# Output and up products that begin with three blocks in step, mixers paced as one sequence, and the residual's load

## The chip, the cores and the metric

The kernel runs on one core of one Trainium2 chip. The metric is the time of one execution on the device in microseconds (us), median over several runs.

## What is computed

The reference is one decoder block over 2048 positions and a width of 1024, in float32. Cut to what matters here:

```python
h = rms_norm(x, norm1_g[l]) * (1 + sc1) + sh1
proj = h @ w_in[l]
...                                    # gated linear attention and dilated attention
mixed = jnp.concatenate([y_gla, y_att], axis=-1)
x = x + g1 * (mixed @ w_out[l])
h = rms_norm(x, norm2_g[l]) * (1 + sc2) + sh2
u = causal_depthwise_conv(h @ w_up[l], conv_w[l], conv_b[l])
u_gate, u_val = jnp.split(u, 2, axis=-1)
x = x + g2 * ((jax.nn.silu(u_gate) * u_val) @ w_down[l])
```

`sh1` to `g2` come from one small product of the condition vector with `w_ada`, 48 blocks of 128 columns.

## The kernel before

The 2048 positions are four chunks (`NCH`) of 512; the width of 1024 is eight channel blocks (`KD`) of 128. Each weight block and each activation is split into a rounded part and a remainder (`hi`, `lo`), and every product of two of them is three matmuls, in `mm3` (L281): hi by hi (L288), lo by hi or hi by lo (L289, L290). A weight block is loaded by the DMA queue of SyncE (SP) into one of two `wraw` buffers (L220), cast by ScalarE into one of three `whi` buffers (L226), and its remainder is formed by VectorE, or by GpSimd for every second up block, into one of three `wlo` buffers (L227). `plan` lists all weight blocks in the order of use, and `weights` keeps casts up to two blocks ahead of the product. The products accumulate in four banks of PSUM (`psg`); the mixers use four others (`psa`).

The stages of a chunk:

- `proj`: normalised input by `w_in`, 26 steps. For the eight blocks of attention heads, `qk` squares the product (L403), casts the squares (L405), forms their remainder on GpSimd (L406) and sums them over a head by a product with a block matrix (L411, L412). The last step of chunks 1 to 3 is a "wide" block W1 that holds all four banks; ScalarE's Tanh (L460) and VectorE (L461) empty them.
- `mix`: the two kinds of attention of the chunk, 68 steps. It reads from and writes to DRAM scratch; the last step of each attention head pair stores its output block (`stage`, L839, store L840).
- `outproj`: loads the eight output blocks of the mixer (L855), casts them (L857) and forms remainders (L859); eight output blocks `out0` to `out7`, each 8 channel blocks of 3 matmuls, gated and added to the residual by VectorE (L865). Then come the sum of squares (`norm_stats`: squares L360, sums L365, a product with `ones` L367, Ln and Exp L369, L370) and `norm_mod` (L380 to L384), which makes the input of `ffn`.
- `ffn`: 44 blocks by `w_up` (gate block f and value block f + 22 in turn), a convolution (L888 to L895), the gate (L899 to L905), and `down`: per group of four f, eight output blocks by `w_down`, added to the residual (L933). The last group of chunks 0 to 2 (group 5, two f) is put off as `tail` and done in the next chunk's `outproj`, between the statistics of the norm and `norm_mod`. The residual of that chunk has by then been stored to DRAM (L937) and is loaded again, block by block (L930), into the four buffers of the tags `y0` and `y1`.

`run` sets the order. Generators are stepped against each other: `beside(a, na, b, nb)` does na steps of a for nb steps of b, then the rest of a. First 27 steps of the projections, which go along with the `w_ada` blocks; then the mixer of chunk c beside what follows:

```python
beside(self.mix(0), 68, gemm, 76)
beside(self.mix(1), 68, chain(self.outproj(0), self.ffn(0)), 86)
```

and so on up to mixer 3 beside chunk 2 at 68 per 90 steps; chunk 3's `outproj` and `ffn` run alone. This is the order of the text only. A scheduler that simulates a timeline then sets the order of each engine's instructions, by what it believes to be ready, and so already moves matmuls of several blocks between each other. Each engine and the DMA queue of SP then work in that order: an instruction that waits holds up what stands behind it.

## Time and profile before

| | |
|---|---|
| median of 3 runs | 2672.51 us (2671.59 to 2675.07) |
| the profiled execution | 2676.88 us |
| its span | 2675.1 us |
| TensorE (PE) busy | 2595.0 us, 97% |
| VectorE (DVE) busy | 1891.1 us, 71% |
| ScalarE (ACT) busy | 1273.2 us, 48% |
| GpSimd (POOL) busy | 512.1 us, 19% |
| granted clock of TensorE | 0.989 |

The span is the time between the first and the last instruction of the profiled execution. Times in the profile are from its start. A row of the timeline gives start, length, engine, line, operation and tiles (written <- read); in brackets stands how long the engine was idle before, and what ended that. A row of the waits gives the total, the number and the longest. TensorE's length of a matmul holds its way through the array, so two that follow each other at full rate start closer together than each is long.

### The profile page before, as it was taken

Reading aid. Unit: us, or ns where it says so; the run is one execution under the profiler, and the core shown is the slowest. Engines: PE = TensorE matmul, PEld = TensorE weight load, DVE = VectorE, ACT = ScalarE, POOL = GpSimd, SP = SyncE. Lnnn points to the kernel's source line nnn. Section 1 sums busy time; section 2 is a strip of 40 time slices with the busy share of each in tenths; the row PEclk is TensorE's granted clock in tenths of the full one; section 3 lists DMA queues with packets and bytes.
Section 4 is the critical chain, followed back from the end, with each engine's and each line's share of the span. In section 5 each row is a group of like instructions: output and inputs, shape, how many; then the busy total and the mean of one; then the engine's idle time right before and its main releaser. Section 6 shows DMA issues by size and latency. Waiting matters only on the chain.

```text
span 2675.1 us, 46823 instructions
## 1 busy us (share of the span) xinstructions
PE 2595.0 (97%) x18152; PEld 2122.1 (79%) x18152; DVE 1891.1 (71%) x3756; ACT 1273.2 (48%) x2607; POOL 512.1 (19%) x308
## 2 busy tenths in 40 slices
PE   5988999999989999999999999999999999999999
PEld 3777878888768888888788788878888888788887
DVE  8676784665676866777887777778777766666665
ACT  3445556656645455443545444445455443433332
POOL 1142451212221311101231111022211110111110
PEclk9999999999989999999999999999999999999999
DMA  7868455554552244447434444643344445323222
GB/s 276 295 212 276 160 173 170 186 188 150 173 175 95 93 126 133 124 125 241 135 100 135 133 133 129 197 156 122 104 141 138 140 132 180 131 95 101 97 95 95
DMA packets 192127, 405.09 MB, mean 151 GB/s; under 512 B 19473, under 2 KB 70434, under 8 KB 190626
## 3 DMA queue, kind: packets, MB, share of 16 engines
q1 hardware_dynamic: 191906, 402.11, 46.0%
q8 instruction: 143, 2.34, 0.4%
q14 instruction: 78, 0.64, 0.1%
HBM read 339.12 MB, written 62.91 MB: 150 GB/s over the span
## 4 chain that ended last, share of the span: by engine, by line
PE 77%; DVE 5%; ACT 3%; DMA 2%; issue 1%; POOL 0%; SPq 0%; DVEq 0%; ACTq 0%; POOLq 0%
PE psg L288 22%; PE psg L289 22%; PE psg L290 22%; PE psa L719 2%; PE psa L699 2%; PE psa L821 2%; PE psa L557 1%; DVE wlo L227 1%; ACT whi L226 1%; PE psa L816 1%; PE psa L735 1%; ACT big L709 1%; PE psa L627 0%; PE psa L628 0%; DMA sq<-y 0%
## 5 line engine op out<-in xcount | busy, mean ns | idle before, releaser
L288 PE MATMUL psg<-hhi,whi 128*128 128x512 f32 x2040 | 808.7, 399 | 15.6 <-ACT hhi L382 9.0
L289 PE MATMUL psg<-hlo,whi 128*128 128x512 f32 x2040 | 805.6, 395 | 6.4 <-DVE hlo L384 5.0
L290 PE MATMUL psg<-hhi,wlo 128*128 128x512 f32 x2040 | 803.9, 395 | 0.0
L226 ACT CAST whi<-wraw 128x1024 fp32r<-128x1024 f32 (+1 forms) x391 | 409.6, 1049 | 402.5 <-PE psg L289 307.5
L227 DVE TENSOR_TENSOR wlo<-wraw,whi 128x1024 fp32r<-128x1024 f32 (+1 forms) x300 | 386.1, 1287 | 150.2 <-ACT whi L226 141.4
L227 POOL TENSOR_TENSOR wlo<-wraw,whi 128x1024 fp32r<-128x1024 f32 x91 | 223.7, 2459 | 1340.8 <-ACT whi L226 1138.9
L288 PEld LDWEIGHTS psg<-hhi,whi 128*128 128x128 f32 x2040 | 386.2, 190 | 104.8 <-ACT hhi L382 12.3
L289 PEld LDWEIGHTS psg<-hlo,whi 128*128 128x128 f32 x2040 | 386.4, 189 | 90.3 <-DVE hlo L384 9.8
L290 PEld LDWEIGHTS psg<-hhi,wlo 128*128 128x128 f32 x2040 | 386.5, 189 | 82.3 <-issue 2.0
L288 PE MATMUL psg<-ghi,whi 128*128 128x512 f32 x704 | 280.1, 398 | 0.0
L289 PE MATMUL psg<-glo,whi 128*128 128x512 f32 x704 | 277.1, 394 | 0.0
L290 PE MATMUL psg<-ghi,wlo 128*128 128x512 f32 x704 | 276.3, 392 | 0.0
L933 DVE SCALAR_TENSOR_TENSOR x<-psg,mod,x 128x512 f32<-128x512 f32 x192 | 142.7, 747 | 124.4 <-PE psg L290 120.2
L889 DVE SCALAR_TENSOR_TENSOR y<-psg,conv_w_sb,y 128x511 f32<-128x511 f32 x176 | 130.9, 744 | 88.2 <-ACT y L888 87.9
L288 PE MATMUL psg<-whi,hhi 128*128 128x512 f32 (+2 forms) x512 | 177.5, 353 | 10.5 <-DVE stg L461 7.0
L289 PE MATMUL psg<-wlo,hhi 128*128 128x512 f32 (+2 forms) x512 | 178.7, 349 | 7.2 <-DVE wlo L227 7.2
L290 PE MATMUL psg<-whi,hlo 128*128 128x512 f32 (+2 forms) x512 | 177.3, 349 | 0.0
L288 PEld LDWEIGHTS psg<-ghi,whi 128*128 128x128 f32 x704 | 132.5, 188 | 32.2 <-issue 4.5
L290 PEld LDWEIGHTS psg<-ghi,wlo 128*128 128x128 f32 x704 | 132.5, 188 | 28.4 <-issue 1.0
L289 PEld LDWEIGHTS psg<-glo,whi 128*128 128x128 f32 x704 | 132.7, 188 | 28.1 <-issue 2.1
L709 ACT ACTIVATE big<-big,nm 128x256 f32<-128x256 f32 (+1 forms) x256 | 122.4, 479 | 47.1 <-DVE nm L724 47.1
L581 POOL TENSOR_TENSOR pt<-kt,pt 128x512 f32<-128x512 f32 x56 | 92.4, 1650 | 264.2 <-ACT pt L578 186.5
(199 smaller groups left out, 3617.7 us busy)
## 6 DMA issues: line engine op xcount, KB each, us to landing
wraw<-in_w_up_dram SPq DMA_DIRECT2D x176, 512.0 KB, 3.3
wraw<-in_w_down_dram SPq DMA_DIRECT2D x88, 512.0 KB, 3.3
wraw<-in_w_ch_dram SPq DMA_DIRECT2D x48, 512.0 KB, 4.2
wada<-in_w_ada_dram SPq DMA_DIRECT2D x40, 512.0 KB, 5.0
v<-v SPq DMA_DIRECT2D x68, 256.0 KB, 5.1
wraw<-in_w_tokw_dram SPq DMA_DIRECT2D x32, 512.0 KB, 3.9
wraw<-in_w_out_dram SPq DMA_DIRECT2D x32, 512.0 KB, 4.0
sq<-in_xT_dram SPq DMA_DIRECT2D x48, 256.0 KB, 3.9
```

Of the source, the lines that this page charges most:

```text
L226: nc.scalar.copy(hi[:, :n], raw[:, :n])
L227: (nc.gpsimd if pool else nc.vector).tensor_tensor(lo[:, :n], raw[:, :n], hi[:, :n].bitcast(F32), op=ALU.subtract)
L288: nc.tensor.matmul(ps, wh, hh, start=first and k == 0, stop=False, skip_group_check=shared)
L289: nc.tensor.matmul(ps, wh, hl, start=False, stop=False, skip_group_check=shared)
L290: nc.tensor.matmul(ps, wl, hh, start=False, stop=k == n - 1, skip_group_check=shared)
L581: nc.gpsimd.tensor_tensor(kh, gk, df, op=ALU.mult)
L699: nc.tensor.matmul(at(i, hh, z), q[H[hh], i * P:(i + 1) * P], key(H[hh], i, z), start=True, stop=True, skip_group_check=True)
L709: nc.scalar.activation(t[:, lo:hi], t[:, lo:hi], AF.Exp, bias=nm[:, hh, g, i:i + 1], scale=2.0 ** -(h + 1), accum_out=dn[:, hh, g, i:i + 1])
L719: nc.tensor.transpose(ps[:n, i * P:(i + 1) * P], part(S[hh], i), self.C("id"))
L821: nc.tensor.matmul(out, lhsT, rhs, start=first[hh], stop=False, skip_group_check=True)
L889: nc.vector.scalar_tensor_tensor(y[:, 1:], ps[:, :T - 1], self.cw[:, 1, b:b + 1], y[:, 1:], op0=ALU.mult, op1=ALU.add)
L933: nc.vector.scalar_tensor_tensor(x1, ps, self.mod[:, 40 + cb:41 + cb], x1, op0=ALU.mult, op1=ALU.add)
```

## The change

Three parts.

The mixers become one sequence, class `Mixers`, that is stepped at a rate: 68/64 steps per step of the projections, and 68/90 per step of every chunk's `outproj` and `ffn`. A mixer no longer ends with its stage: when mixer 0 is done beside the projections, mixer 1 starts there. `upto` makes sure that a mixer is done before its output is used. Chunk 0's mixer output is loaded and cast (`mixed`) inside the last step of the last projection, before its banks are emptied.

`three` makes the first three blocks of the output product, and of the up product, together: the loop over the channel blocks is outermost, the three blocks lie inside it, the third two channel blocks behind. The squares of the norm are taken block by block in the loop over output blocks.

The residual of the put-off down product is loaded by `spare_x1`: four blocks at the start of the next chunk's `outproj`, and one more after each of the first four blocks is stored.

```diff
+class Mixers:
+    def __init__(self, mix):
+        self.gs = [mix(c) for c in range(NCH)]
+        self.at, self.acc = 0, 0.0
+    def one(self):
+        done = object()
+        while self.at < NCH and next(self.gs[self.at], done) is done:
+            self.at += 1
+    def step(self, rate):
+        self.acc += rate
+        while self.acc >= 1.0:
+            self.acc -= 1.0
+            self.one()
+    def upto(self, c):
+        while self.at <= min(c, NCH - 1):
+            self.one()
...
+    def three(self, names, hs):
+        pss = [self.pg() for _ in range(3)]
+        ws = [self.weights(*n, ahead=2 - i) for i, n in enumerate(names)]
+        for k in range(KD + 2):
+            for b, ps in enumerate(pss):
+                j = k - 2 * (b == 2)
+                if 0 <= j < KD:
+                    self.mm3(ps, ws[b][j:j + 1], hs[j:j + 1], j == 0, True)
+            if k in (2, 5):
+                yield
+        self.psd = pss
+    def outproj(self, c):
+        hs = self.hs_out.pop(c, None) or self.mixed(c)
         x1 = self.load_x(c)
+        if c:
+            for _ in range(4):
+                self.spare_x1(c - 1)
+        acc = None
+        yield from self.three([("w_out", cb) for cb in range(3)], hs)
         for cb in range(KD):
-            ps = self.pg()
-            self.mm3(ps, self.weights("w_out", cb), hs)
+            if cb < 3:
+                ps = self.psd[cb]
+            else:
+                ps = self.pg()
+                self.mm3(ps, self.weights("w_out", cb), hs)
             nc.vector.scalar_tensor_tensor(x1[cb], ps, self.mod[:, 16 + cb:17 + cb], x1[cb], op0=ALU.mult, op1=ALU.add)
-            yield
+            acc = self.square(acc, x1[cb])
+            if cb >= 2:
+                yield
-        rstd = self.norm_stats(lambda k: x1[k])
+        rstd = self.norm_end(acc)
...
+    def spare_x1(self, c):
+        cb = len(self.late)
+        t = self.up.tile([P, T], F32, name="x1", tag=f"y{cb % 2}")
+        self.nc.sync.dma_start(t, self.D[c]["x1"][cb])
+        self.late.append(t)
...
     def ffn(self, c):
+        yield from self.three([("w_up", b) for b in (0, NF, 1)], h2)
...
     def down(self, c, gj, pgs):
                 if gj == 5 and defer:
-                    x1 = self.up.tile([P, T], F32, name="x1", tag=f"y{cb % 2}")
-                    nc.sync.dma_start(x1, self.D[c]["x1"][cb])
+                    x1 = self.late[cb]
...
                     nc.sync.dma_start(A["outT"][c, cb], x1)
+                    if defer and cb < 4:
+                        self.spare_x1(c)
...
-            yield from self.proj(c, hs.pop(), (lambda: begin(c + 1)) if c < 3 else None, () if c else done)
+            yield from self.proj(c, hs.pop(), (lambda: begin(c + 1)) if c < 3 else into_out, () if c else done)
+
+        def into_out():
+            mixers.upto(0)
+            self.hs_out[0] = self.mixed(0)
...
-        beside(self.mix(0), 68, gemm, 76)
-        beside(self.mix(1), 68, chain(self.outproj(0), self.ffn(0)), 86)
-        beside(self.mix(2), 68, chain(self.outproj(1), self.ffn(1)), 86)
-        beside(self.mix(3), 68, chain(self.outproj(2), self.ffn(2)), 90)
-        for _ in chain(self.outproj(3), self.ffn(3)):
-            pass
+        mixers = Mixers(self.mix)
+        for _ in gemm:
+            mixers.step(68 / 64)
+        for c in range(NCH):
+            for _ in chain(self.outproj(c), self.ffn(c)):
+                mixers.step(68 / 90)
+            mixers.upto(c + 1)
```

What the scheduler makes of it stands in three places. The number of matmuls is the same. TensorE's order is the same up to the end of chunk 1's first wide block (879 instructions) and from the middle of chunk 2's put-off down product to the end (1541 instructions).

**First listing.** TensorE at the start of chunk 0's output product, before. `psg_7411`, `psg_7443` and `psg_7490` are the banks of out0, out1 and out2; `hhi_7385` is the cast mixer output of channel block 6 and `hhi_7391` that of block 7; L557 are score matmuls of mixer 1.

```order
L290 MATMUL psg_7490<-hhi_7385,wlo_7415 128x512
L557 MATMUL psa_7522<-kt_7475 32x32 x16
L557 MATMUL psa_7540<-kt_7475 32x32 x16
L557 MATMUL psa_7598<-pt_7562,pt_7563 32x32 x8
L557 MATMUL psa_7609<-pt_7562,pt_7563 32x32 x8
L557 MATMUL psa_7692<-pt_7624,pt_7625 32x32 x16
L557 MATMUL psa_7710<-pt_7624,pt_7625 32x32 x16
L288 MATMUL psg_7411<-hhi_7391,whi_7260 128x512
L288 MATMUL psg_7443<-hhi_7391,whi_7299 128x512
L288 MATMUL psg_7490<-hhi_7391,whi_7414 128x512
L289 MATMUL psg_7411<-hlo_7393,whi_7260 128x512
```

Before, all three output blocks stop ahead of channel block 7, and score matmuls stand there. The same engine after: the last rows of W1 (banks `psg_7548` and `psg_7549`, written in turn with two others), small matmuls of mixer 1, and the first row of out0 (`psg_7819`).

```order
L315 MATMUL psg_7548<-whi_7589,hlo_5754 128x512
L313 MATMUL psg_7549<-whi_7589,hhi_5752 128x512
L314 MATMUL psg_7549<-wlo_7590,hhi_5752 128x512
L315 MATMUL psg_7549<-whi_7589,hlo_5754 128x512
L688 MATMUL psa_7849<-consts_sb_458,pt_7793 128x128 x4
L688 MATMUL psa_7857<-consts_sb_458,pt_7798 128x128
L574 MATMUL psa_7901<-consts_sb_458,s16_7893 128x128 x3
L688 MATMUL psa_7857<-consts_sb_458,pt_7798 128x128
L574 MATMUL psa_7901<-consts_sb_458,s16_7893 128x128
L688 MATMUL psa_7857<-consts_sb_458,pt_7798 128x128 x2
L591 MATMUL psa_7944<-kt_7892 32x32 x3
L313 MATMUL psg_7819<-hhi_7725,whi_7643 128x512
```

Out0 now begins behind W1 and a few small matmuls of the next mixer. A few rows further on, at channel block 2 of out0 and out1 (`psg_7820`) and block 0 of out2 (`psg_7821`):

```order
L313 MATMUL psg_7819<-hhi_7737,whi_7643 128x512
L314 MATMUL psg_7819<-hlo_7739,whi_7643 128x512
L315 MATMUL psg_7819<-hhi_7737,wlo_7644 128x512
L313 MATMUL psg_7820<-hhi_7737,whi_7695 128x512
L314 MATMUL psg_7820<-hlo_7739,whi_7695 128x512
L315 MATMUL psg_7820<-hhi_7737,wlo_7696 128x512
L313 MATMUL psg_7821<-hhi_7725,whi_7824 128x512
L314 MATMUL psg_7821<-hlo_7727,whi_7824 128x512
```

The blocks go in turn by channel block, out2 behind the others, and no score matmul stands between them up to the end of all three.

**Second listing.** The DMA queue of SP between the store of mixer 0's last output block (L840) and its load for the output product (L855), before. `rg` is the scratch that W1 is stored to, `x` the residual.

```order
L840 DMA y_123<-stage 128x512
L465 DMA rg_154<-stg 128x512
L342 DMA x<-in_xT_dram 128x512 x2
L465 DMA rg_154<-stg 128x512
L342 DMA x<-in_xT_dram 128x512
L465 DMA rg_154<-stg 128x512
L342 DMA x<-in_xT_dram 128x512
L220 DMA wraw<-in_w_out_dram 128x1024
L682 DMA v_9577<-v_135 128x128 x2
L754 DMA v_9838<-v_135 128x512
L754 DMA v_9838<-v_122 128x512
L855 DMA sq<-y_123 128x512
```

The load stands eleven rows behind the store. After, around the last loads of mixer 0's output (L890); L499 stores W1:

```order
L462 DMA k_160<-o_7427 128x512
L890 DMA sq<-y_123 128x512 x2
L245 DMA wraw<-in_w_out_dram 128x1024
L890 DMA sq<-y_123 128x512
L245 DMA wraw<-in_w_out_dram 128x1024
L890 DMA sq<-y_123 128x512
L245 DMA wraw<-in_w_out_dram 128x1024
L367 DMA x<-in_xT_dram 128x512 x3
L499 DMA rg_154<-stg 128x512
L367 DMA x<-in_xT_dram 128x512
L691 DMA y_136<-stage 128x4x128
```

The loads of the mixer's output now stand ahead of the stores of W1 and of the residual's loads, and the store of mixer 0's last block (L874) stands 24 rows ahead of this piece.

**Third listing.** The same queue at the put-off down product of chunk 2, in chunk 3's output product, before: L935 stores a finished block, L930 loads the residual (`x_150` is the scratch).

```order
L935 DMA out_dram<-x_23008 128x512
L935 DMA out_dram<-x_23019 128x512
L935 DMA out_dram<-x_23030 128x512
L930 DMA x_23058<-x_150 128x512
L935 DMA out_dram<-x_23041 128x512
L930 DMA x_23069<-x_150 128x512
L930 DMA x_23080<-x_150 128x512
L930 DMA x_23091<-x_150 128x512
L935 DMA out_dram<-x_23058 128x512
```

After (L1011 stores, L939 loads):

```order
L1011 DMA out_dram<-x_22709 128x512
L1011 DMA out_dram<-x_22711 128x512
L1011 DMA out_dram<-x_22713 128x512
L939 DMA x_23018<-x_150 128x512
L1011 DMA out_dram<-x_22715 128x512
L939 DMA x_23029<-x_150 128x512
L939 DMA x_23040<-x_150 128x512
L939 DMA x_23051<-x_150 128x512
L1011 DMA out_dram<-x_23018 128x512
```

Nothing has moved: the load of the fifth block stands behind the stores of the first three, as before.

More of the change, by code (lines that the diff above doesn't have):

```diff
@@ L354, in norm_stats, with square, norm_end @@
     def norm_stats(self, src):
-        nc = self.nc
         acc = None
         for k in range(KD):
-            sq = self.tmp.tile([P, T], F32, name="sq", bufs=3)
-            nc.scalar.activation(sq, src(k), AF.Square)
-            if acc is None:
-                acc = self.tmp.tile([P, T], F32, name="rstd", bufs=2)
-                nc.vector.tensor_copy(acc, sq)
-            else:
-                nc.vector.tensor_tensor(acc, acc, sq, op=ALU.add)
+            acc = self.square(acc, src(k))
+        return self.norm_end(acc)
+    def square(self, acc, x):
+        nc = self.nc
+        sq = self.tmp.tile([P, T], F32, name="sq", bufs=3)
+        nc.scalar.activation(sq, x, AF.Square)
+        if acc is None:
+            acc = self.tmp.tile([P, T], F32, name="rstd", bufs=2)
+            nc.vector.tensor_copy(acc, sq)
+        else:
+            nc.vector.tensor_tensor(acc, acc, sq, op=ALU.add)
+        return acc
+    def norm_end(self, acc):
+        nc = self.nc
         ms = self.pa()
@@ L847, in mix, with mixed @@
             yield from self.attn(c, hp)
-    def outproj(self, c):
-        nc, A = self.nc, self.A
+    def mixed(self, c):
+        nc = self.nc
         hs = []
@@ L860, in outproj @@
             hs.append((hi, lo))
-        x1 = self.load_x(c)
-        for cb in range(KD):
-            ps = self.pg()
-            self.mm3(ps, self.weights("w_out", cb), hs)
+        return hs
+    def three(self, names, hs):
[10 more added lines that the diff above has]
+    def outproj(self, c):
+        nc, A = self.nc, self.A
+        hs = self.hs_out.pop(c, None) or self.mixed(c)
+        x1 = self.load_x(c)
+        if c:
[3 more added lines that the diff above has]
+        yield from self.three([("w_out", cb) for cb in range(3)], hs)
+        for cb in range(KD):
+            if cb < 3:
+                ps = self.psd[cb]
+            else:
+                ps = self.pg()
+                self.mm3(ps, self.weights("w_out", cb), hs)
             nc.vector.scalar_tensor_tensor(x1[cb], ps, self.mod[:, 16 + cb:17 + cb], x1[cb], op0=ALU.mult, op1=ALU.add)
-            yield
+            acc = self.square(acc, x1[cb])
+            if cb >= 2:
+                yield
         self.x1[c] = x1
-        rstd = self.norm_stats(lambda k: x1[k])
+        rstd = self.norm_end(acc)
         yield from self.tail
         self.h2[c] = self.norm_mod(lambda k: x1[k], rstd, self.G2, self.mod[:, 24:32], True)
+    def spare_x1(self, c):
[3 more added lines that the diff above has]
+        self.late.append(t)
     def ffn(self, c):
@@ L884, in ffn @@
                         b = f + NF * half
-                        ps = self.pg()
-                        self.mm3(ps, self.weights("w_up", b), h2)
+                        if f + NF * half in (0, NF, 1):
+                            ps = self.psd[2 * f + half]
+                        else:
+                            ps = self.pg()
+                            self.mm3(ps, self.weights("w_up", b), h2)
                         y = self.up.tile([P, T], F32, name=f"y{half}")
@@ L896, in ffn @@
                         ys.append(y)
-                        yield
+                        if b not in (0, NF):
+                            yield
                     th = self.up.tile([P, T], F32, name="th", bufs=1)
@@ L909, in ffn @@
                 if grp is None and c < NCH - 1:
-                    self.tail = d
+                    self.tail, self.late = d, []
                 else:
@@ L921, in down @@
         defer = c < NCH - 1
+        if gj == 5 and defer and not self.late:
+            raise AssertionError("the residual has not been loaded")
         for q in range(1024 // cols):
@@ L943, in run @@
         self.scratch()
-        self.x1, self.h2, self.tail = {}, {}, ()
+        self.x1, self.h2, self.tail, self.hs_out, self.late = {}, {}, (), {}, []
         xs = self.load_x(0)
```

## The prediction

> **What bounds the kernel now.** I read the page first, then a table of stretches, then the waits of TensorE in those stretches, then the timeline of the one stretch that stood out.
>
> ```profile
> span 2675.1 us, 46823 instructions
> ...
> PE 2595.0 (97%) x18152; PEld 2122.1 (79%) x18152; DVE 1891.1 (71%) x3756; ACT 1273.2 (48%) x2607; POOL 512.1 (19%) x308
> ```
>
> TensorE is busy for 97% of the span, and the change leaves the number of matmuls alone. So what can be won is TensorE's idle time, 2675.1 - 2595.0 = 80.1 us, and the time that it runs at a lower clock. The stretches say where that lies (columns: length, busy us of each engine, granted clock, DMA).
>
> ```profile
> core 0: us, PE busy (x) PEld busy (x) DVE busy (x) ACT busy (x) POOL busy (x), PEclk, DMA share, GB/s
> 0.00:234.00 234.00, 186.03 (x970) 148.56 (x971) 173.78 (x285) 103.11 (x159) 56.72 (x45) 0.96 0.77 264
> 234.00:735.00 501.00, 490.72 (x3810) 406.35 (x3809) 325.22 (x668) 300.19 (x631) 143.41 (x101) 0.99 0.54 178
> 735.00:775.00 40.00, 35.95 (x423) 28.45 (x422) 29.88 (x40) 14.67 (x30) 15.38 (x13) 0.91 0.67 232
> 775.00:825.00 50.00, 44.65 (x328) 35.63 (x327) 34.17 (x54) 25.30 (x45) 8.36 (x5) 0.90 0.24 81
> 825.00:2299.00 1474.00, 1469.61 (x11028) 1200.55 (x11026) 1093.42 (x2360) 697.56 (x1581) 236.09 (x125) 1.00 0.43 138
> 2299.00:2675.00 376.00, 368.02 (x1603) 302.57 (x1601) 234.65 (x353) 132.41 (x164) 52.13 (x22) 0.99 0.30 100
> ```
>
> The first 234 us hold 48.0 us of the idle time and the last 376 us hold 8.0. In both, TensorE's instructions stand in the same order before and after. Between them lie 10.3 us (projections of chunks 1 to 3 beside mixer 0), 4.1 us (start of the output product of chunk 0), 5.4 us (norm of chunk 0) and 4.4 us in the 1474 us that follow. So 24 us are within reach of this change, and the three in-step starts of chunks 1 to 3 lie where there is next to nothing to win. The waits of TensorE, first of 735 to 825 us, then of 234 to 735 us (total, times, longest):
>
> ```profile
> PE psa L367 <- DVE rstd L365: 2.9, 1, 2.9
> PE psg L288 <- ACT hhi L857: 2.7, 1, 2.7
> PE psa L557 <- POOL pt L581: 1.4, 1, 1.4
> PE psa L557 <- DVE pt L580: 1.3, 1, 1.3
> PE psg L289 <- DVE hlo L384: 1.2, 1, 1.2
> ```
>
> ```profile
> PE psa L412 <- POOL sqr L406: 4.3, 3, 1.9
> PE psg L288 <- DVE stg L461: 3.1, 2, 2.7
> PE psg L288 <- ACT stg L464: 2.4, 1, 2.4
> ```
>
> The wait on L857 is the output product's: L857 casts the mixer's output. TensorE's timeline there:
>
> ```profile
> 749.47 0.39 PE L289 MATMUL psg<-hlo,whi 128*128 128x512 f32 x1
> 749.70 0.39 PE L290 MATMUL psg<-hhi,wlo 128*128 128x512 f32 x1
> ...
> 752.61 0.76 PE L557 MATMUL psa<-pt 64*32 64x32 f32 x64 [1.38 <-POOL pt L581]
> 756.03 1.65 PE L288 MATMUL psg<-hhi,whi 128*128 128x512 f32 x3 [2.66 <-ACT hhi L857]
> 757.47 0.63 PE L289 MATMUL psg<-hlo,whi 128*128 128x512 f32 x1
> 757.90 0.63 PE L290 MATMUL psg<-hhi,wlo 128*128 128x512 f32 x1
> ```
>
> And the last output block of mixer 0 on its way (VectorE, then the DMA queue's store and load, then ScalarE's cast):
>
> ```profile
> 734.83 1.09 DVE L839 TENSOR_TENSOR stage<-psa,stage 128x512 f32<-128x512 f32 x1 [0.72 <-ACT stage L838]
> ```
>
> ```profile
> 741.36 0.32 SPq L840 DMA_DIRECT2D y<-stage  x1
> ...
> 749.73 0.32 SPq L855 DMA_DIRECT2D sq<-y  x1
> ```
>
> ```profile
> 755.36 0.62 ACT L857 CAST hhi<-sq 128x512 fp32r<-128x512 f32 x1 [1.27 <-DMA sq<-y]
> ```
>
> Mixer 0 ends at 735.9 us, when the projections end too, and its last block needs 755.36 - 735.92 = 19.4 us to come back from DRAM. By 749.9 TensorE has done seven of eight channel blocks of three output blocks, in an order that the scheduler chose by itself, and waits.
>
> **The change, part by part.**
>
> *Mixers paced as one sequence, chunk 0's mixer output loaded before the projections end.* The rate beside the projections goes from 68/76 to 68/64, so mixer 0 ends 12 steps earlier, and its eight loads and casts stand ahead of the evacuation of the last projection (second order listing). The path of 19.4 us is then off TensorE's path. This removes 2.66 us of waiting on L857. It also removes the 1.38 us on L581: those score matmuls were pulled forward to fill this hole, and now stand between whole output blocks. Then comes the clock: from 756.03 on nine matmuls stand 757.90 - 757.47 = 0.43 us apart instead of 749.70 - 749.47 = 0.23, which is 9 x 0.20 = 1.8 us. Together 5.8 us. The score matmuls themselves are only moved.
>
> Are short gaps enough to slow the clock? The tail of chunk 2's down product shows gaps of 0.41, 0.74 and 0.53 us, then matmuls of 0.63 us instead of 0.39.
>
> ```profile
> 2303.79 0.49 PE L288 MATMUL psg<-hhi,whi 128*128 128x512 f32 x1 [0.41 <-ACT hhi L382]
> 2305.03 0.49 PE L288 MATMUL psg<-hhi,whi 128*128 128x512 f32 x1 [0.74 <-DVE x L933]
> 2306.06 0.50 PE L288 MATMUL psg<-hhi,whi 128*128 128x512 f32 x1 [0.53 <-ACT whi L226]
> ...
> 2307.13 0.63 PE L288 MATMUL psg<-hhi,whi 128*128 128x512 f32 x1
> ...
> 2310.09 0.40 PE L288 MATMUL psg<-hhi,whi 128*128 128x512 f32 x1
> 2310.33 0.39 PE L289 MATMUL psg<-hlo,whi 128*128 128x512 f32 x1
> ```
>
> The Trainium skill, page "TensorE: Matmul & The Clock Gate", section "Why this matters for your kernels", asks only for no idle gaps above about 3 us between bursts of matmuls; by it no gap here would slow the clock, and the sum would be 1.8 us smaller. The trace disagrees twice (1.38 and 2.66 us, or 0.41 to 0.74 us, each followed by matmuls of 0.63 us), so the 1.8 us stay in.
>
> What is late next at this place: the three banks of PSUM that the output blocks need. The last projection holds all four, and ScalarE and VectorE empty them:
>
> ```profile
> 734.59 1.12 ACT L460 ACTIVATE stg<-psg 128x512 f32<-128x512 f32 x2
> ```
>
> ```profile
> 735.83 1.28 DVE L461 SCALAR_TENSOR_TENSOR stg<-stg,psg 128x512 f32<-128x512 f32 x2
> ```
>
> That is about 0.6 + 0.7 = 1.3 us a bank. The first bank has its last matmul nine matmuls before the end (9 x 0.23 = 2.1 us, first listing), so it is free in time, and the others follow 0.6 to 0.7 us apart, while out0 alone has six matmuls (1.4 us) ahead of out1. I take 0; with no cover it costs the 2.7 us of the L461 row above.
>
> *The denser mixers* add 12 mixer steps to the 501 us of projections and take them out of later products. No row shows that density. Bound from below: all 10.3 us of idle time there are filled. From above: the head chains wait for ScalarE and VectorE; there are 24 of them:
>
> ```profile
> L405 ACT CAST sqr<-sq 128x512 fp32r<-128x512 f32 x24 | 15.0, 624 | 0.4
> ```
>
> Three of them wait now, 4.3/3 = 1.4 us each (L412). If half of all 24 did, it would cost 12 x 1.4 = 17 us. ScalarE is busy 300/501 = 60% and VectorE 325/501 = 65%, far from full, so I lean to a small gain, 1 us: more scores stand behind some waits.
>
> *Output blocks in step, channel block outermost.* In chunks 1 to 3 the mixer's output is long there, so no wait is removed. What it adds: three weight blocks are held at once, and the fourth can be cast only when out0 is through.
>
> ```profile
> L226 ACT CAST whi<-wraw 128x1024 fp32r<-128x1024 f32 (+1 forms) x391 | 409.6, 1049 | 402.5 <-PE psg L289 307.5
> L227 DVE TENSOR_TENSOR wlo<-wraw,whi 128x1024 fp32r<-128x1024 f32 (+1 forms) x300 | 386.1, 1287 | 150.2 <-ACT whi L226 141.4
> ```
>
> ```profile
> L865 DVE SCALAR_TENSOR_TENSOR x<-psg,mod,x 128x512 f32<-128x512 f32 x32 | 23.9, 748 | 44.0 <-PE psg L290 42.0 <-DMA x<-x 1.9
> ```
>
> Cast and remainder take 1.05 + 1.29 = 2.3 us. The cover is what of out1 and out2 is left then: 3 + 9 = 12 matmuls, 2.7 us, and out3's first two matmuls need only the cast. It fits by 0.4 us; were VectorE one instruction late (0.75 us, L865), three chunks would lose about 1 us together. I take 0. The three up blocks are in the same step order before: the scheduler had made it. 0 too. The squares move into the loop in the text, but stood there already; the norm's path from the last block to `rstd` keeps its operations.
>
> *The norm of chunk 0* keeps its 2.9 us on L365. The two waits behind it (1.3 on L580, 1.2 on L384) depend on which mixer steps stand in VectorE's queue; different ones now. Between 0 and -2.5: I take -1.
>
> *The residual four blocks ahead.* The four loads stand in the DMA queue where they stood (third listing), because the scheduler had already hoisted them; blocks 5 to 8 wait for the same four buffers. 0, and the 0.74 us on L933 stays.
>
> Sum: -5.8 - 1 - 1 = -7.8 us. The profiled execution took 2676.88 us (span plus 1.8), so 2669.1 for one like it; its time is 4.4 us over the median of the runs, 2672.51, from which I forecast 2672.5 - 7.8 = 2664.7. What a measurement of this kernel can tell from no change is about 0.2%, 5.3 us, so faster means below 2667.2.
>
> **The rivals.** *More is filled.* The denser mixers also fill half of the projections' 10.3 us (5.2), and half of the slow clock that follows such gaps, about 2.5 more: 2664.7 - 7.7 = 2657. For it: these waits are short, and more scores are at hand. Against: most are on banks of PSUM and on POOL, which more mixer work doesn't free. 0.18.
>
> *The wait is replaced.* The output product now starts right behind the last projection and waits for its banks, 2.7 us and the slow clock again, 1.8: 2664.7 + 4.5 = 2669, no change that can be told. It decides if ScalarE's Tanh of the first bank is queued behind a late cast of the mixer's output. 0.18.
>
> *Slower.* Beside the denser mixers half the 24 head chains make TensorE wait 1.4 us, +17: 2664.7 + 17 = 2682. It happens in the projections of chunks 1 to 3, where TensorE stands in order at the product with the block matrix of L412, and it outweighs the gain from 6 chains on (6 x 1.4 = 8.4 against 7.8). 0.15.
>
> *Interleaving costs.* Four in-step output starts each lose one stretch of slow clock, 4 x 1.8 = 7.2: 2672, no change. The Trainium skill, the same page, section "Loop structure matters more than you think", wants all channel blocks of one output tile in a row. Against it: the up blocks in step at 2310.09 and 2310.33 stand 0.23 us apart. 0.03.
>
> **How the numbers follow.** My own case has 0.46, with 2658 to 2671 around it; 0.33 of that is faster, 0.13 within 0.2%. Faster: 0.33 + 0.18 = 0.51; within: 0.13 + 0.18 + 0.03 = 0.34; slower: 0.15. The range is 2653 to 2681: below the first rival by its unfilled half, above to just short of the slower one.
>
> **What would show it.** Right: no wait of TensorE on the cast of the mixer's output, a clock of about 1.0 at the start of chunk 0's output product, out0 to out2 0.23 us apart; chunk 3 and the last 376 us as before. Wrong: waits on the banks right behind the last projection; a projection stage with more than 15 us idle between 234 us and the output product; or gaps at out3 in chunks 1 to 3.

## The result, and the profile after

| | before | after |
|---|---|---|
| median | 2673.79 us (6 runs, 2670.37 to 2676.94) | 2695.03 us (6 runs, 2690.80 to 2702.21) |
| the profiled execution | 2676.88 us | 2702.21 us |
| its span, granted clock | 2675.1 us, 0.989 | 2700.4 us, 0.985 |

The changed kernel is slower: the ratio is 1.0081, 95% interval 1.0065 to 1.0097, some 21 us. The profiled execution is 7 us over its own median, so its 25.3 us of extra span overstate the difference. Line numbers have moved: L313 to L315 are the three matmuls of `mm3` (L288 to L290 before), L446 the head chain's product (L412), L495 the emptying of W1's banks (L461), L769 the first scores of an attention head (L735), L252 the weights' remainder (L227), L401 and L416 the norm (L367, L382).

The busy times on the page of the changed kernel:

```profile
PE 2602.8 (96%) x18152; PEld 2127.5 (79%) x18152; DVE 1889.9 (70%) x3756; ACT 1269.3 (47%) x2605; POOL 510.9 (19%) x308
```

There are as many matmuls as before. TensorE is idle for 17.5 us more (97.6 against 80.1) and busy for 7.8 us more; since the work is the same, the latter is put down to the clock. The same table of stretches as in the prediction, with the projections cut into three (columns: length, busy us of PE, PEld, DVE, ACT, POOL, granted clock, DMA):

```profile
0.00:235.00 235.00, 184.29 (x988) 146.79 (x988) 171.12 (x282) 101.74 (x158) 60.23 (x46) 0.96 0.77 261
235.00:391.00 156.00, 150.03 (x1412) 124.89 (x1413) 118.47 (x173) 92.50 (x177) 57.54 (x41) 0.97 0.57 186
391.00:580.00 189.00, 175.83 (x1300) 145.33 (x1298) 118.13 (x316) 118.54 (x289) 40.16 (x29) 0.98 0.54 173
580.00:769.00 189.00, 183.77 (x1593) 152.32 (x1594) 117.58 (x239) 103.41 (x216) 57.12 (x43) 0.97 0.53 175
769.00:809.00 40.00, 40.00 (x320) 32.47 (x321) 29.05 (x35) 14.39 (x27) 14.82 (x11) 1.00 0.50 165
809.00:859.00 50.00, 43.83 (x427) 33.37 (x426) 37.56 (x55) 25.20 (x41) 13.63 (x7) 0.90 0.17 54
859.00:2324.00 1465.00, 1456.76 (x10517) 1189.63 (x10515) 1063.27 (x2307) 680.92 (x1539) 215.00 (x112) 1.00 0.43 138
2324.00:2700.00 376.00, 368.31 (x1604) 302.70 (x1602) 234.71 (x353) 132.60 (x164) 52.39 (x22) 0.99 0.30 101
```

The kernel before, the same three parts of its projections:

```profile
233.00:384.00 151.00, 142.45 (x1363) 117.61 (x1363) 109.73 (x154) 87.73 (x163) 60.12 (x41) 0.98 0.55 184
384.00:556.00 172.00, 171.67 (x1126) 141.85 (x1126) 109.21 (x247) 110.60 (x250) 41.12 (x30) 0.99 0.55 179
556.00:735.00 179.00, 176.95 (x1322) 147.24 (x1323) 107.28 (x272) 102.45 (x222) 42.18 (x31) 0.99 0.52 172
```

Idle time is length less PE busy. In the projections it went from 8.6 + 0.3 + 2.0 = 10.9 us to 6.0 + 13.2 + 5.2 = 24.4 us, and the clock fell by 0.01 to 0.02 over 534 us, by these rounded figures about 7 us more. The start of chunk 0's output product gained: idle 4.05 us before, none now, at a clock of 1.00 instead of 0.91. The norm lost 0.8 us, the 1465 us behind it 3.9 us. The first 235 us, where TensorE's order is unchanged, show 3.4 us more, which no edit explains and another execution need not show. The waits of TensorE from 391 to 769 us (total, times, longest) name what stood behind the 18.4 us:

```profile
PE psg L313 <- DVE stg L495: 4.5, 2, 3.2
PE psa L769 <- DMA qf<-q: 4.2, 2, 3.9
PE psa L591 <- DVE kt L600: 2.3, 1, 2.3
PE psa L769 <- issue: 1.9, 1, 1.9
PE psa L753 <- DVE big L818: 1.7, 2, 0.8
PE psa L798 <- DVE xm L795: 1.6, 1, 1.6
PE psa L855 <- DVE big L198: 1.2, 1, 1.2
PE psa L574 <- DMA s<-la: 0.5, 1, 0.5
PE psa L446 <- POOL sqr L440: 0.3, 1, 0.3
PE psa L445 <- ACT sqr L439: 0.2, 1, 0.2
```

Only the last two rows are the head chain of the rival *Slower*, and the first is the emptying of W1's banks. The others are steps of the mixer itself, 13.4 us together: TensorE works in a fixed order and stands at a step of mixer 0 whose input is not there yet. The longest one, and what it does to the clock (272 columns a matmul; two stand 0.23 us apart behind the wait, and some 0.12 us from 424.27 on):

```profile
419.11 1.00 PE L769 MATMUL psa<-kt,qf 64*32 64x32 f32 x64 [3.89 <-DMA qf<-q]
...
420.66 0.43 PE L315 MATMUL psg<-whi,hlo 128*128 128x272 f32 x1
420.88 0.43 PE L313 MATMUL psg<-whi,hhi 128*128 128x272 f32 x1
...
424.27 0.28 PE L313 MATMUL psg<-whi,hhi 128*128 128x272 f32 x1
```

The DMA queue shows why. The load of `qf` is issued at 412.19, behind loads of x for the statistics (L1050) and a store of the mixer (L691), and it lands only 6.8 us later. Of the 16 such loads in this execution half land within 3.9 us (least, median, most):

```profile
408.48 0.98 SPq L691 DMA_DIRECT2D y<-stage  x2
...
412.19 0.33 SPq L702 DMA_DIRECT2D qf<-q  x1
```

```profile
DMA to landing us min/median/max: 2.9/3.9/7.1
```

A good part of this longest wait is thus one slow load. In e2 and e4 below, where TensorE's order is the same up to this place, the load lands within 4.4 us and TensorE waits 0.7 and 0.9 us.

At the output product of chunk 0 the forecast held. It begins right behind the last projection with no wait on the cast, and its matmuls stand 0.23 us apart from the second on:

```profile
768.88 0.50 PE L313 MATMUL psg<-hhi,whi 128*128 128x512 f32 x1
769.22 0.40 PE L314 MATMUL psg<-hlo,whi 128*128 128x512 f32 x1
769.45 0.40 PE L315 MATMUL psg<-hhi,wlo 128*128 128x512 f32 x1
```

### The profile page after: what moved, and what is told of

It reads as the page before. It is cut to its first block, busy times and chain, and to the rows that moved or that the text cites. A ratio compares the mean times of both kernels' runs of the same rounds, so it can differ in the third digit from the quotient of the medians.

```text
span 2700.4 us, 46860 instructions
## 1 busy us (share of the span) xinstructions
PE 2602.8 (96%) x18152; PEld 2127.5 (79%) x18152; DVE 1889.9 (70%) x3756; ACT 1269.3 (47%) x2605; POOL 510.9 (19%) x308
## 4 chain that ended last, share of the span: by engine, by line
PE 66%; DVE 6%; ACT 2%; issue 1%; DMA 1%; POOL 0%; SPq 0%; DVEq 0%; ACTq 0%; POOLq 0%
PE psg L313 19%; PE psg L315 19%; PE psg L314 19%; PE psa L753 2%; PE psa L733 2%; PE psa L855 2%; PE psa L591 1%; DVE wlo L252 1%; PE psa L769 0%; DVE y L963 0%; PE psa L850 0%; ACT big L743 0%; ACT whi L251 0%; PE psa L662 0%; DVE y L967 0%
## 5 line engine op out<-in xcount | busy, mean ns | idle before, releaser
L313 PE MATMUL psg<-hhi,whi 128*128 128x512 f32 x2040 | 810.7, 400 | 16.9 <-ACT hhi L416 12.9
L315 PE MATMUL psg<-hhi,wlo 128*128 128x512 f32 x2040 | 806.7, 396 | 3.5 <-DVE wlo L252 2.8
L252 DVE TENSOR_TENSOR wlo<-wraw,whi 128x1024 fp32r<-128x1024 f32 (+1 forms) x300 | 387.4, 1292 | 176.1 <-ACT whi L251 153.5
L252 POOL TENSOR_TENSOR wlo<-wraw,whi 128x1024 fp32r<-128x1024 f32 x91 | 223.6, 2457 | 1388.8 <-ACT whi L251 1135.8
L313 PEld LDWEIGHTS psg<-hhi,whi 128*128 128x128 f32 x2040 | 388.1, 190 | 108.5 <-ACT hhi L416 16.4
L315 PEld LDWEIGHTS psg<-hhi,wlo 128*128 128x128 f32 x2040 | 387.8, 190 | 87.5 <-DVE wlo L252 3.5
L313 PE MATMUL psg<-ghi,whi 128*128 128x512 f32 x704 | 279.2, 397 | 0.0
L315 PE MATMUL psg<-ghi,wlo 128*128 128x512 f32 x704 | 275.3, 391 | 0.0
L313 PE MATMUL psg<-whi,hhi 128*128 128x512 f32 (+2 forms) x512 | 177.8, 353 | 10.7 <-DVE stg L495 7.2
L315 PE MATMUL psg<-whi,hlo 128*128 128x512 f32 (+2 forms) x512 | 178.2, 349 | 0.0
L313 PEld LDWEIGHTS psg<-ghi,whi 128*128 128x128 f32 x704 | 132.1, 188 | 31.2 <-issue 3.3
L315 PEld LDWEIGHTS psg<-ghi,wlo 128*128 128x128 f32 x704 | 132.2, 188 | 28.6 <-issue 1.0
L962 ACT ACTIVATE y<-psg,conv_b_sb,conv_w_sb 128x512 f32<-128x512 f32 x176 | 135.8, 774 | 9.6 <-DVE glo L980 9.1
```

The lines of the kernel that those rows point to most:

```text
L252: (nc.gpsimd if pool else nc.vector).tensor_tensor(lo[:, :n], raw[:, :n], hi[:, :n].bitcast(F32), op=ALU.subtract)
L313: nc.tensor.matmul(ps, wh, hh, start=first and k == 0, stop=False, skip_group_check=shared)
L315: nc.tensor.matmul(ps, wl, hh, start=False, stop=k == n - 1, skip_group_check=shared)
L962: nc.scalar.activation(y, ps, AF.Identity, bias=self.cb[:, b:b + 1], scale=self.cw[:, 2, b:b + 1])
```

## The experiments

The theory after the result was P: the new pacing costs the time, since mixer 0's steps now meet the projections so that TensorE stands at them. It was narrowed to D (the density of the steps decides) and A (the pairing decides: which step meets which part of the projections). The rivals: the products in step cost the time (T), the early load does (L), or single late loads do (Q). Each run is compared with the kernel before on the same chip; 0.1% is 2.7 us.

**The change, taken apart.** Four runs: the changed kernel at the old rate beside the projections; the kernel before with the new pacing alone; the changed kernel without pacing and early load; and the changed kernel with only mixer 0 denser, the others paced as before.

```diff
 e1   mixers.step(68 / 64)  ->  mixers.step(68 / 76)
 e2   (before) beside(self.mix(0), 68, gemm, 76) ...  ->  Mixers, 68 / 64, then 68 / 90
 e3   Mixers, into_out  ->  beside(...) as before, no into_out
 e4   Mixers  ->  beside(self.mix(0), 68, gemm, 64), the rest as before; into_out kept
```

e1: 

> The changed kernel with one number put back: beside the projections the mixers step at 68/76 instead of 68/64. Theory P (the denser mixers beside the projections make TensorE wait, in order, at the mixers' own steps: 17 us more between 391 and 580 us of the profile after, 7 more up to the output product): 2668 to 2680, the waits on L769, L753 and L798 between 391 and 769 us mostly gone; the wait for mixer 0's last output block may come back, up to 6 us. Rival T (the three blocks in step cost the time): as after, 2690 to 2700.

e2: 

> The kernel before with the pacing alone: the mixers as one sequence at 68/64 and 68/90, nothing in step, the mixer's output loaded where it was, the residual as before. Theory P: 2688 to 2700, with waits of TensorE at mixer steps beside the projections. Rival T: 2665 to 2676, since the costly part is not there.

e3: 

> The changed kernel with the pacing of before, mixer by mixer, and without the early load of chunk 0's mixer output: what stays is the three blocks in step, the squares in the loop and the residual. Theory P: 2668 to 2679, like before. Rival T: 2690 to 2700.

e4: 

> The changed kernel, but mixer by mixer again: mixer 0 at 68/64 until it is done, 12 steps ahead of the projections' end, no step of mixer 1 beside the projections; later rates as before; the early load of chunk 0's mixer output stays. Theory P, by the density of mixer 0: 2680 to 2692, the loss of some 17 us stays and the wait for the last output block is gone. Rival M (it is mixer 1's start beside the projections, and mixers running over the ends of stages, that cost): 2663 to 2672.

Measured: e1 1.0041 (1.0028 to 1.0053), e2 1.0041 (1.0028 to 1.0053), e3 1.0017 (1.0008 to 1.0026), e4 1.0035 (1.0021 to 1.0048). P holds for e4 (2684.7) and, half a microsecond under its range, for e2 (2687.5), and T has a rest: e3, 2681.0, is over P's 2679 and far under T's 2690. e1 lies between all ranges. So the pacing carries more than half, the rest of the change about 5 us, and slowing the pace beside the projections alone takes away only half of the loss. In e1 the projections are nearly as before again: 502.0 us from 236 to 738 us, with 489.3 us of PE busy, so 12.7 us idle (10.9 before). What is left of its loss shows behind them: between 801 and 1249 us TensorE waits 5.9 us for casts and remainders of the norm and 3.4 us for a load of the mixer (L574), where the kernel before waits 1.2 and 0. The 17 us that P names are the difference in length of two stretches, 189 and 172 us; their idle time differs by 13 us.

**A slower step up, with and without the early load.** If density decides, 68/72 costs a part of 68/64.

```diff
-        beside(self.mix(0), 68, gemm, 76)
+        beside(self.mix(0), 68, gemm, 72)
```

e5 (with the early load): 

> The kernel before with two edits alone: mixer 0 runs at 68 steps to 72 of the projections' (68 to 76 before), and chunk 0's mixer output is loaded and split in the last projection; no three in step, no squares in the loop, residual as before. Theory D (the loss lies in how densely mixer 0's steps stand beside the projections, and falls with the rate): the wait ahead of the output product goes (about -5 us) and a third to a half of the +10 to +17 of 68/64 stays: 2671 to 2681 beside a kernel before of about 2675. Rival L (the early load itself costs, whatever the rate, since its loads and splits stand among the last projection's): 2683 or more.

e10 (without): 

> The kernel before with one number changed: mixer 0 at 68 steps to 72, nothing loaded early. The run with the early load as well took 1.0050. If the early load is what costs (its eight loads and splits stand ahead of the last W1's evacuations on VectorE): 2675 to 2679 beside 2675. If the denser or newly paired mixer costs, whatever is loaded: 2682 to 2688, with idle of TensorE of 10 us more than before's between 234 and 735 us.

Measured: e5 1.0050 (1.0034 to 1.0065), e10 1.0055 (1.0042 to 1.0068). D in its simple form falls: a third of the step up costs no less than the whole one did in e4. The 2690.5 us of e5 are what L had named, but L falls by e10: 72 costs as much without the early load, 2690.8 us, over both ranges named for it. The projections of e10 hold 518.10 - 495.57 = 22.5 us of idle time at a clock of 0.97, and the longest waits there (total, times, longest) lie again at the mixer's steps (L816, L735, L614):

```profile
233.40:751.50 518.10, 495.57 (x3836) 411.13 (x3836) 325.29 (x671) 300.44 (x632) 137.39 (x99) 0.97 0.55 180
```

```profile
PE psa L816 <- ACT big L171: 3.1, 1, 3.1
PE psa L735 <- DVE wlo L227: 3.1, 1, 3.1
PE psa L614 <- POOL pt L600: 2.9, 1, 2.9
```

e5 shows one thing more: its output product doesn't wait for the cast but 4.2 us for a bank (L461), the wait that the rival *The wait is replaced* had named.

```profile
PE psg L288 <- DVE stg L461: 4.2, 1, 4.2
```

**The pairing alone.** The same density, with the free places between the mixer's steps elsewhere: the accumulator of the first `beside` starts at 0.25, 0.5 or 0.75.

```diff
-def beside(a, na, b, nb):
+def beside(a, na, b, nb, acc=0.0):
...
-        beside(self.mix(0), 68, gemm, 76)
+        beside(self.mix(0), 68, gemm, 76, 0.5)
```

e9 (0.5): 

> The kernel before with one number changed: the accumulator that paces mixer 0 beside the projections starts at 0.5 and not at 0, so mixer 0 keeps 68 steps to 76 and each free place between steps falls elsewhere. Theory D (density alone decides): within 3 us of the kernel before. Theory A (which step of the mixer meets which part of the projections decides, so that any new pairing costs): 5 us or more over it, with new waits of TensorE at the mixer's own steps between 234 and 735 us.

e15 (0.25): 

> The kernel before, the accumulator that paces mixer 0 starts at 0.25 (0 in the kernel before; at 0.5 it came to 1.0035). Theory A (the pairing of the mixer's steps with the projections' parts decides, and the kernel before has a good one): 2678 to 2690. If 0.5 was an unlucky case and most pairings at this density do as well as before's: 2673 to 2678.

e16 (0.75): 

> As the run at 0.25, with 0.75. Theory A: 2678 to 2690. If most pairings at this density do as well as before's: 2673 to 2678.

Measured: 0.25 gives 1.0009 (1.0000 to 1.0018), 0.5 gives 1.0035 (1.0021 to 1.0048), 0.75 gives 0.9988 (0.9979 to 0.9997). So the pairing alone moves the time from 3 us under to 9 us over the kernel before, and A's "any new pairing costs" is too strong: of the three, 0.5 and, by a little, 0.25 lie in A's ranges, and 0.75 gained. At 0.5 the idle time in the projections is 507.30 - 491.05 = 16.3 us, of which 10.9 were there before; the mixer's own steps among the new waits are L556, L835 and L631:

```profile
235.60:742.90 507.30, 491.05 (x3809) 408.06 (x3810) 327.22 (x669) 300.11 (x633) 136.08 (x100) 0.98 0.53 176
```

```profile
PE psa L556 <- DVE kt L567: 2.1, 1, 2.1
PE psa L835 <- DVE pt L800: 2.0, 2, 1.8
PE psa L631 <- ACT pt L170: 1.3, 1, 1.3
```

**Late loads, or slow chains.** e8 issues the loads of a pair of heads one step earlier in the changed kernel; e12 leaves 16 small operations of VectorE a pair of heads out of it, e13 out of the kernel before.

```diff
 e8   +        if hp < 3:
 e8   +            self.pre[c, hp + 1] = self.heads(c, hp + 1)
 e12, e13
-                nc.vector.tensor_scalar(s4[hh][:, i, z:], s4[hh][:, i, z:], f[:, hh, 1, i:i + 1], None, op0=ALU.mult)
...
-                nc.vector.tensor_scalar(sn[hh][:, i, z:], sn[hh][:, i, z:], f[:, hh, 2, i:i + 1], None, op0=ALU.mult)
```

e8: 

> The changed kernel, but the loads of heads 1 to 3 of each chunk's attention are issued in the head before's last step, one step earlier. Theory Q (TensorE stands because the loads of q, k and v come too late for a head that follows this closely): the 4.2 us of waits for q between 391 and 769 us go with the slow clock behind them, and the time falls by 5 to 12 us from the changed kernel's 2695. Theory V (the engines' chains within the mixer's steps, VectorE's above all, are too long for the denser pace, and a load that comes earlier only moves the wait to the next of them): within 4 us of the changed kernel.

e12: 

> The changed kernel without the 16 tensor_scalar of each attention head that weight the scores of the second and third window (left out: that part of the softmax's merge), some 5.3 us of VectorE a head. Theory V (TensorE's new waits between 391 and 769 us come from VectorE's share of the mixer's chains, which is too long for the denser pace): idle of TensorE there falls from 18 us to under 9, and the time by 8 us or more from the changed kernel's 2695. Theory A or a chain through the other engines: idle there within 4 us of the changed kernel's, the time within 4 us.

e13: 

> The kernel before without the same 16 tensor_scalar of each attention head (left out: that part of the softmax's merge), the control of the run that left them out of the changed kernel, which came to 1.0014. If VectorE's chains bind only under the denser pace, the kernel before gains 4 us or less: 2671 to 2676. If they cost the kernel before as much, it gains some 15 us: 2658 to 2664, and the run on the changed kernel says nothing on the pace.

Measured: e8 1.0078 (1.0064 to 1.0092), as the changed kernel. Q falls: the waits on q are gone, and others of the same kind stand in their place, the longest new one here (236 to 767 us, total, times, longest), with 19.4 us of idle time in all:

```profile
PE psa L738 <- DVE md L744: 2.6, 1, 2.6
```

e12 1.0014 (1.0005 to 1.0023), 15 us under the changed kernel's 2695; e13 1.0000 (0.9992 to 1.0009). VectorE's busy time falls by 70 us in the one and 67 in the other, some 4.3 us a pair of heads. That is worth nothing at the old pace and 15 us of the changed kernel's time, as V said. V's size for the idle time was too bold: from 386 to 757 us it is 8.4 + 3.2 = 11.6 us, not under 9, against 18.4 in the changed kernel.

```profile
386.00:571.00 185.00, 176.58 (x1304) 146.26 (x1301) 110.26 (x285) 118.93 (x289) 40.39 (x29) 0.98 0.55 178
571.00:757.00 186.00, 182.78 (x1599) 151.40 (x1600) 111.41 (x208) 103.23 (x217) 59.61 (x43) 0.98 0.55 179
```

Even this says less for V than it seems. The 3.9 us at 419.11 are more than half of that gain, and they are not VectorE's: e12 comes to the same instruction, the 2503rd of TensorE in both, with no wait, before the first of the operations that it leaves out (at 457.6 us in the changed kernel):

```profile
412.61 0.76 PE L769 MATMUL psa<-kt,qf 64*32 64x32 f32 x64
```

In the two profiled executions e12 is 6.5 us ahead here, gains 5.5 us more up to chunk 0's output product (756.83 against 768.88), and 8.9 us behind it. And leaving the operations out gives TensorE another order, in e12 from 459 us on and in e13 from 498 us on, so a luckier pairing (A) isn't excluded. V fits, and isn't shown.

**The later pace.**

```diff
+        beside(self.mix(0), 68, gemm, 76)
+        mixers = Mixers(self.mix)
+        mixers.at = 1
+        for c in range(NCH):
+            for _ in chain(self.outproj(c), self.ffn(c)):
+                mixers.step(68 / 90)
+            mixers.upto(c + 1)
```

e14: 

> The kernel before with mixer 0 as it was (68 to 76), and mixers 1 to 3 as one sequence at 68 to 90 that runs over the stages' ends; nothing else. If the pace beside the projections carries the whole loss of the pacing (+11 in the run with the pacing alone): 2674 to 2679. If the sequence beside the output, up and down products carries some of it: 2680 to 2684.

Measured: 1.0044 (1.0031 to 1.0057), more than the rival allowed: the later pace alone costs as much as the whole pacing did (e2). The terms don't add up. Here mixer 1 ends only with its stage, and the start of chunk 1's output product waits as chunk 0's did before (1225 to 1310 us; before: none of these):

```profile
PE psa L565 <- DMA s<-la: 2.2, 1, 2.2
PE psg L313 <- ACT hhi L882: 1.4, 1, 1.4
```

The changed kernel doesn't have these, since its mixer 1 begins earlier. Chunk 2 has others, none over 1.1 us: its idle time from 1751 to 2254 us is 7.0 us, where the kernel before has 1.7. Together with chunk 1 (5.2 against 1.9) that is 8.6 of some 12 us; the profiled execution of e14 (2682.50 us) was the fastest of its five, whose median is 2688.19, so where the rest lies stays open.

**The products in step.** From the run without pacing (e3), the up or the output products back in a row; then the output products in step alone, on the kernel before.

e6: 

> The earlier run without the new pacing and the early load (which took 1.0017 of the time before), and w_up's products one after the other again: left are the three output products in step, the squares in the loop and the residual four ahead. If the output products carry the +5 us: 2679 to 2683 beside 2676; if the up products carry them: 2674 to 2677.

e7: 

> The earlier run without the new pacing and the early load, and w_out's products one after the other again: left are the three up products in step, the squares in the loop and the residual four ahead. If the output products carry the +5 us: 2674 to 2677 beside 2676; if the up products carry them (their third product's weights are split later, and the norm's channel blocks are wanted by three products at once): 2679 to 2683. Both runs at 2679 or more would put it on the squares or the residual's loads.

e17: 

> The kernel before with the three output products in step, channel block outermost, and nothing else (the squares in the loop give the same order on every engine, so they drop out). If the output products in step carry the +5 us that the changed kernel costs without its pacing: 2678 to 2682 beside 2675.5. If it is the residual's loads or the two together: 2674 to 2677.

Measured: e6 1.0019 (1.0010 to 1.0028), e7 1.0005 (0.9996 to 1.0013), e17 1.0021 (1.0013 to 1.0030). The output products in step carry it: 5.6 us by themselves. The up products, with the residual's loads beside them, can't be told from nothing. e17's trace shows two places. The first is out3 of chunk 1, and likewise 0.76 us at 1767.8 in chunk 2: its third matmul waits for the remainder of its weights.

```profile
1260.28 0.50 PE L290 MATMUL psg<-hhi,wlo 128*128 128x512 f32 x1 [0.77 <-DVE wlo L227]
```

The second is the norm of chunk 0: 4.0 and 2.8 us of waits instead of 2.9, 1.3 and 1.2, and a clock of 0.83 from 775 to 825 us, which was 0.90:

```profile
PE psa L367 <- DVE rstd L365: 4.0, 1, 4.0
PE psg L288 <- ACT hhi L382: 2.8, 1, 2.8
```

```profile
775.00:825.00 50.00, 43.15 (x365) 34.00 (x365) 34.18 (x53) 23.35 (x37) 9.12 (x5) 0.83 0.24 77
```

That is 2 x 0.77 + 6.8 - 5.4 = 2.9 us of waits and 0.07 x 50 = 3.5 us of clock, 6.4 us in one execution, beside the measured 5.6.

**What the forecast wanted to gain, alone.** e11 loads seven of chunk 0's eight blocks ahead of mixer 0's last step; e19 does it at the phase 0.75.

```diff
+            if b == 1 and c == NCH - 1:
+                self.hs_out[0] = self.mixed(0, range(KD - 1))
```

e11: 

> The kernel before, mixer 0 as it was (68 to 76), with one move: the first seven blocks of chunk 0's mixer output are loaded and split behind the last W1's evacuations, ahead of the mixer's last step, so that their loads no longer queue on SP behind the store of that step's result; the eighth is loaded where it was. If the wait of the output product is what the forecast took it for, a queue behind one store: 2668 to 2673 beside 2675. If the wait for the store is only moved to the eighth block: 2674 to 2677.

e19: 

> The kernel before with the two edits that came out at or below it: the pacing's accumulator starts at 0.75 (0.9988 alone) and the first seven blocks of chunk 0's mixer output are loaded ahead of the mixer's last step (1.0002 alone). If the two add nothing to each other: 0.9985 to 0.9993 of before, 2671.5 to 2673.5. If the other pairing lets the early loads take the wait of the output product away: 2666 to 2670. If a new order of the instructions loses the 0.75's gain: 2675 or more.

Measured: e11 1.0002 (0.9993 to 1.0010), e19 0.9989 (0.9979 to 0.9999). The wait is moved to the eighth block, 2.5 us and 2.7 before; it is the last step's own way through DRAM, not a queue ahead of seven others.

```profile
PE psg L288 <- ACT hhi L860: 2.5, 1, 2.5
```

e19 adds nothing to e16. The fastest kernel here is the one before with one number changed, 0.12% or 3 us under it (e16), from which e19 can't be told.

## Why the prediction was wrong

It gave 2664.7 us with a range up to 2681; measured were 2695.0. By its own steps:

- *The y wait, -5.8.* Right in place and near in size: the stretch went from 4.05 us idle at 0.91 to none at 1.00, which is 4.05 + 0.09 x 40 = 7.6 us. But in these runs it came only together with an earlier end of mixer 0.
- *The denser mixers, -1.* This is the step that failed. "ScalarE is busy 60% and VectorE 65%, far from full, so I lean to a small gain": in the profiled execution the projections lost 13.5 us to waits and about 7 to the clock, and putting this one rate back (e1) took 0.40% off, some 11 us. Busy shares didn't speak to it. TensorE comes, in its fixed order, to a step of the mixer whose input isn't there yet. Why the inputs come late stays open between VectorE's part of the chain (e12 beside e13) and the pairing of the steps (e9, e16). Nor has the rate one price: e4 beside e3 (rate and early load) is 3.7 us slower, and e2 no slower than e14, which has the old rate. The bound above, +17, was near in size, but was drawn from the head chains of L412, which are hardly late: 2.8 us in all from 235 to 769 us, against 4.3 before. The rival *Slower* thus had the right stretch and about its price, by the wrong wait, at 0.15, and its 2682 is still 13 us short.
- *Output blocks in step, 0.* Mis-sized: 5.6 us (e17). Of its two parts the prediction had the first as a condition (the remainder of out3's weights fits by 0.4 us, "were VectorE one instruction late ... about 1 us"); in e17 0.77 us a chunk were lost in two chunks. The other, a later norm of chunk 0, was not seen. In the changed kernel out3 doesn't wait, but out2 does, in chunk 2, for 2.78 us (the listing at the end): it is the 21st matmul of the output product, the third of out2. Three blocks in step want the third one's remainder that early, and VectorE, busy with the mixer, the gate and the down product, begins it 2.6 us after the cast is done at 1786.79 (the row below). The prediction priced the fourth block's weights and not the third's. e8 and e12 have the same wait (2.58 and 2.77 us), and e2, which has no blocks in step, doesn't.

```profile
1789.34 1.22 DVE L252 TENSOR_TENSOR wlo<-wraw,whi 128x1024 fp32r<-128x1024 f32 x1
```

- *The norm of chunk 0, -1.* Wrong sign: 6.2 us idle, 0.8 more than before.
- *Banks late at out0, 0.* Right in the changed kernel; in e5 it happened, 4.2 us.
- *Up blocks, squares, residual, 0.* Right as far as e7 can tell (1.0005, 0.9996 to 1.0013).
- *The pace of the later mixers* was given no term beyond "takes them out of later products". The 1465 us from 859 on have 8.2 us idle instead of 4.4, and e14 shows that this pace alone can cost 0.44%. Why the single costs (e2 0.41%, e10 0.55%, e14 0.44%, e17 0.21%) don't add up is not settled; that each edit sets the pairing anew is argued from e9, e15 and e16, not shown for each.
- *The Trainium skill's rules.* "Loop structure matters more than you think", in the page "TensorE: Matmul & The Clock Gate", shows as good the nest in which one output tile's channel blocks follow each other, so that matmuls stay back to back. Here the matmuls in step stay back to back too, 0.23 us apart; e17's 1.0021 comes through a late remainder and a later norm, so the price of the rival *Interleaving costs*, 7.2 us, is near e17's 5.6 by luck.

Of the signs named in advance, "a projection stage with more than 15 us idle between 234 us and the output product" was near in the worst stage (13.2) and exceeded by the three together (24.4); "gaps at out3" did not come in the changed kernel, whose gap is at out2, but did in e3 and e17.

## What to carry to other kernels

Where two streams of work are stepped against each other and each engine keeps a fixed order, don't price a change of pace by the busy shares of the engines: look for the steps of the inner stream whose input may not be there when the outer one's order comes to them. Change the phase alone first: if the same density at another phase moves the time by 0.3%, the gain of any re-pacing under that size is luck of the pairing, and each step of the change has to be measured by itself. A wait for a stream's own last step didn't go by loading the earlier ones sooner (e11). It went when the stream ended earlier, and that had its own price.

## What the runs showed of the hardware

A wait under 3 us can be followed by matmuls at half rate for longer than it lasted. In the changed kernel at out2 of chunk 2:

```profile
1790.61 0.79 PE L315 MATMUL psg<-hhi,wlo 128*128 128x512 f32 x1 [2.78 <-DVE wlo L252]
...
1792.75 0.63 PE L314 MATMUL psg<-hlo,whi 128*128 128x512 f32 x1
...
1796.73 0.39 PE L315 MATMUL psg<-hhi,wlo 128*128 128x512 f32 x1
```

After 2.78 us of waiting, matmuls stand 0.43 us apart until 1796.2 and 0.23 from then on: 5.6 us at half rate, so the wait cost about 2.8 us a second time. The 3.89 us at 419.11 cost 1.7 us again in the same way (17 matmuls, each 0.10 us later). But this is no fixed price. In the kernel before, two waits of 1.43 us at the same line, in chunks 1 and 2, end differently:

```profile
1294.43 0.45 PE L557 MATMUL psa<-pt 64*32 64x32 f32 x32 [1.43 <-ACT rstd L369]
...
1297.19 0.39 PE L289 MATMUL psg<-glo,whi 128*128 128x512 f32 x1
```

```profile
1800.49 0.45 PE L557 MATMUL psa<-pt 64*32 64x32 f32 x32 [1.43 <-ACT rstd L369]
...
1803.55 0.63 PE L289 MATMUL psg<-glo,whi 128*128 128x512 f32 x1
```

Behind the first the matmuls stay 0.23 us apart, behind the second they stand 0.43 us apart until 1804.8. The short gaps at the tail of chunk 2 that the prediction shows were followed by slow matmuls in the kernel before; in e2 gaps of 0.73 and 0.53 us at the same place were not. What decides it these traces don't tell, so a term for the clock behind a single wait is in part luck, the prediction's 1.8 us too. The Trainium skill, same page, section "Why this matters for your kernels", puts the limit at gaps of about 3 us; the 2.78 us here are close to it, and the 1.43 us at 1800.49, as the shorter gaps of the prediction, disagree. Over whole runs the granted clock is lower too: 0.9868 on average over the changed kernel's six runs, 0.9887 over the 27 runs of the kernel before beside e14; 0.0019 x 2600 = 4.9 us of busy time, as an estimate.
